# A two-block transformer with a mixture of experts on one core: retention on 128-token tiles, a spread slot product, and fetched tokens in place of one-hot gathers

## The chip, the core and the metric

The kernel runs on one core of a Trainium2 chip. The metric is device time in microseconds of one execution; the profile is of one such execution. PE is the matmul engine, PEld its weight loads, DVE, ACT and POOL the vector, scalar and general engines, SP the engine that issues most of the DMAs.

## The reference

Two blocks follow each other on one sequence of 512 tokens of width 1024. The first mixes tokens by windowed attention and by retention, then by a convolution, each followed by attention over a memory. The second has three branches and then a mixture of 32 experts, two per token. The parts that the change touches:

```python
def retention(q, k, v):                      # 4 heads, key and value width 128, CHUNK = 64
    intra = jnp.exp(log_gamma[:, None, None] * jnp.abs(idx[:, None] - idx[None, :]))
    k_decay = jnp.exp(log_gamma[:, None] * (CHUNK - 1 - idx)[None, :])
    q_decay = jnp.exp(log_gamma[:, None] * (idx + 1.0)[None, :])
    chunk_decay = jnp.exp(log_gamma * CHUNK)
    sc = jnp.einsum('bnihd,bnjhd->bnhij', qc, kc) * intra
    o_intra = jnp.einsum('bnhij,bnjhe->bnihe', sc, vc)
    kv = jnp.einsum('bnjhd,bnjhe,hj->nbhde', kc, vc, k_decay)
    _, states = lax.scan(lambda state, kv_c: (state * chunk_decay + kv_c, state), 0, kv)
    o = o_intra + jnp.einsum('bnihd,nbhde,hi->bnihe', qc, states, q_decay)
    return o * lax.rsqrt(jnp.mean(o * o, axis=-1, keepdims=True) + EPS)

def hierarchical_moe(h, ...):                # router, then per expert: tokens in, tokens out
    weights, expert_idx = ...                # two experts of each token, and their weights
    def run_block(toks, e):
        xb = x_pad[toks]
        a = jax.nn.silu(xb @ w_gate_e[e]) * (xb @ w_up_e[e])
        return a @ w_down_e[e]
    y = yb.reshape(R, D) * row_w[:, None]
    return jax.ops.segment_sum(y, row_tok)
```

## The kernel before

Features lie on partitions and tokens on the free axis; a big product is three float32r matmuls (high and low parts of weights and data, L321 to L323). Weights come from HBM by SP into two buffers `raw`, and ACT and DVE split each half (`w`, L250 and L251, three buffers). Up to the experts a scheduler sets the order of all engines from the program and its priorities; in the experts (`moe`) PE's order is as written, and the other engines are still scheduled. Every engine runs its list in order.

**Retention** (`retention`, L572) runs for two heads after the first half of its projections (the calls are in the loop `for half in range(2)`) and for two after the second. On a tile of 128 tokens the scores are one product (L577), masked by `intra` to two blocks of 64; `kd` is k transposed (L584) and scaled on ACT (L586). Then come 7 products of 64 rows for the chunk states (L592), 7 steps on DVE that chain the states (L597), 8 products of 64 columns with them (L602), 4 inner products (L608), and the normalization, after which `retention_out` transposes `oc` (L627). The gate projection of the same half (`ew` group 3 or 7) stands beside it on PE. In the second half ACT and DVE also prepare the memory (`ms`, L253 and L254, from POOL's product L418) and the first weights of the next stage (`w` from `in_wkv`).

**The experts.** Each of the 32 experts has 64 slots in the first round; expert j and j + 16 share a tile of 128 rows. A turn i of `moe` handles tiles a = 2i and b = 2i + 1: `gu` (L1398, gate and up, 32 matmuls of 512 columns on 64 of them at a time), `act`, `flip` (transposes of the 128 x 256 result, L1412), `down` (L1424), and `combine` of the turn before (L1445), which adds the rows back to their tokens. Weights of a turn are twelve loads of 1 MB into a ring of twelve tiles `ew` (four for `gu` of a, four for b, two and two for `down`); each is loaded again as soon as PE is through with it. The tokens of a turn come by `gather(i)`, called between `flip` and `down` of b in the turn before (and once ahead of the loop): either 64 float32r matmuls of the kept activations `h2` with one-hot matrices `oh` that DVE builds (L1347, L1348, L1364), or, for i in `FETCH` = 3, 5, 7, rows of the copy `hd` in HBM that POOL fetched by two indirect DMAs of 128 rows each (`fetch`, L1332) and that PE transposes (L1358). `slot_rows` (L1281) makes for each slot its token, its weight and its norm: 8 steps of five small DVE operations and one float32 product of 48 columns (L1295). It stands after `gu` of tile 0, and `act` of tile 0 needs its result `rh`; the fetches need its `sti`.

## Time and profile before

| | |
|---|---|
| median of 3 runs | 1682.16 us (1681.27 to 1683.08) |
| profiled execution, its own time | 1682.74 us |
| its span, first to last instruction | 1680.8 us |
| PE busy over the span | 1622.0 us (97%) |
| 157 to 252 us (retention of both halves): PE busy | 90.1 of 95 us |
| 252 to 1358 us: PE busy | 1100.2 of 1106 us |
| 1358 to 1681 us (experts and end): PE busy | 287.2 of 323 us |
| bytes moved, whole span | 237.7 MB, 141 GB/s |
| bytes per second, 1358 to 1681 us | 318 GB/s, DMA engines busy 0.79 |

A row of the timeline gives start, length, engine, line, operation, output and inputs, shape and count; what stands in brackets is the idle time of the engine ahead of it and who ended it. Matmuls overlap: a length is longer than the distance to the next start, and it is the distance that counts. A float32 matmul shows as two instructions. A granted clock of 1.00 is 2.4 GHz, one of 0.50 is 1.2 GHz.

### The profile page before, as it was taken

The page shows a single profiled execution, that of the slowest core. Times are in us where ns is not written, and L with a number is a line of the kernel's source. Part 1 is how long each engine was busy: PE and PEld are TensorE (multiplying, and loading weights), DVE is VectorE, ACT ScalarE, POOL GpSimd, SP SyncE. Part 2 cuts the span into 40 slices and gives each one's busy share as a digit, 9 for nine tenths or more (in the row PEclk, how much of TensorE's full clock was granted, in tenths as well). Part 3 has the DMA queues.
Part 4 walks back from the last instruction along what each step waited for, and adds up shares of the span by engine and source line. Part 5 has one row for each costly group of instructions (what it writes and reads, how often), then busy time and mean ns, then how long its engine had stood idle before and what let it go on. Part 6 is the DMA issues. An engine that isn't in the chain of part 4 may idle for free. (4 is left out here: it accounts for less than half of the span.)

```text
span 1680.8 us, 20780 instructions
## 1 busy us (share of the span) xinstructions
PE 1622.0 (97%) x8174; PEld 1239.3 (74%) x8174; DVE 917.3 (55%) x1745; ACT 588.8 (35%) x1036; POOL 117.7 (7%) x104
## 2 busy tenths in 40 slices
PE   7999999999999999999999999999999968999995
PEld 6757769888888889888877777888888854545542
DVE  5575755545555465555795554475445453434335
ACT  5443234435322234434545443245333311111112
POOL 0000200000011120000030000000111200000001
PEclk9999989999999999999999999999999978999998
DMA  6211125220322235230231112242432367899981
GB/s 205 100 51 51 51 79 197 101 75 30 108 88 101 101 116 185 103 124 26 100 110 52 52 58 95 94 163 84 177 125 101 91 231 317 354 382 369 397 361 52
DMA packets 43368, 237.73 MB, mean 141 GB/s; under 512 B 6128, under 2 KB 11120, under 8 KB 17152
## 3 DMA queue, kind: packets, MB, share of 16 engines
q1 hardware_dynamic: 41088, 228.93, 36.6%
q0 software_dynamic: 2176, 7.41, 1.3%
q8 instruction: 66, 1.08, 0.3%
q14 instruction: 38, 0.31, 0.1%
HBM read 230.03 MB, written 6.29 MB: 141 GB/s over the span
## 5 line engine op out<-in xcount | busy, mean ns | idle before, releaser
L250 ACT ACTIVATE w<-raw 128x1024 fp32r<-128x1024 f32 (+2 forms) x242 | 233.9, 968 | 398.5 <-PE mm L323 354.9
L321 PE MATMUL mm<-xg,w 128*128 128x512 f32 x864 | 342.0, 396 | 9.7 <-ACT xg L253 8.0
L251 DVE TENSOR_TENSOR w<-raw,w 128x1024 fp32r<-128x1024 f32 (+2 forms) x242 | 280.5, 1160 | 124.0 <-ACT w L250 122.8
L322 PE MATMUL mm<-xg,w 128*128 128x512 f32 x864 | 341.0, 395 | 0.0
L323 PE MATMUL mm<-xg,w 128*128 128x512 f32 x864 | 340.5, 394 | 0.0
L321 PEld LDWEIGHTS mm<-xg,w 128*128 128x128 f32 x864 | 163.1, 189 | 45.3 <-ACT xg L253 8.0
L323 PEld LDWEIGHTS mm<-xg,w 128*128 128x128 f32 x864 | 163.1, 189 | 35.6 <-issue 3.0
L322 PEld LDWEIGHTS mm<-xg,w 128*128 128x128 f32 x864 | 163.1, 189 | 34.7 <-issue 2.5
L322 PE MATMUL mm<-y,w 128*128 128x512 f32 x448 | 175.3, 391 | 0.0
L323 PE MATMUL mm<-y,w 128*128 128x512 f32 x448 | 174.1, 389 | 0.0
L321 PE MATMUL mm<-y,w 128*128 128x512 f32 x448 | 174.0, 391 | 0.0
L1398 PE MATMUL pgu<-ew,xT 128*64 128x512 f32 x512 | 115.6, 605 | 0.0
L321 PEld LDWEIGHTS mm<-y,w 128*128 128x128 f32 x448 | 83.8, 188 | 18.1 <-ACT y L250 1.2
L323 PEld LDWEIGHTS mm<-y,w 128*128 128x128 f32 x448 | 84.1, 188 | 17.3
L322 PEld LDWEIGHTS mm<-y,w 128*128 128x128 f32 x448 | 84.1, 188 | 17.0 <-DVE y L251 0.4
L1398 PEld LDWEIGHTS pgu<-ew,xT 128*64 128x64 f32 x512 | 36.5, 139 | 72.9 <-issue 71.8
L1445 PE MATMUL py<-ys,comb 128*128 128x512 f32 x256 | 62.4, 397 | 0.0
L1424 PE MATMUL py<-ew,aT 128*64 128x512 f32 x256 | 58.1, 595 | 0.7 <-ACT aT L1414 0.7
L1445 PEld LDWEIGHTS py<-ys,comb 128*128 128x128 f32 x256 | 46.8, 188 | 16.1 <-issue 5.7
L1405 DVE SCALAR_TENSOR_TENSOR eth<-eth,pgu 128x256 f32<-128x256 f32 x16 | 6.7, 421 | 94.2 <-ACT eth L1404 94.2
L1404 ACT ACTIVATE eth<-pgu,rh 128x256 f32<-128x256 f32 x16 | 7.6, 475 | 139.8 <-PE pgu L1398 124.3
L1447 DVE TENSOR_TENSOR merged<-py,merged 128x512 f32<-128x512 f32 x64 | 44.1, 690 | 10.6 <-PE py L1445 10.1
(438 smaller groups left out, 2499.4 us busy)
## 6 DMA issues: line engine op xcount, KB each, us to landing
ew<-in_egu_dram SPq DMA_DIRECT2D x64, 1024.0 KB, 8.5
ew<-in_edn_dram SPq DMA_DIRECT2D x32, 1024.0 KB, 10.2
raw<-in_wkv_dram SPq DMA_DIRECT2D x20, 1024.0 KB, 4.8
raw<-in_ow_dram SPq DMA_DIRECT2D x16, 1024.0 KB, 4.7
raw<-in_ew_dram SPq DMA_DIRECT2D x12, 1024.0 KB, 4.8
raw<-in_w2gate_dram SPq DMA_DIRECT2D x12, 1024.0 KB, 4.8
raw<-in_wq_dram SPq DMA_DIRECT2D x8, 1024.0 KB, 4.8
raw<-in_wo_dram SPq DMA_DIRECT2D x8, 1024.0 KB, 4.8
```

Source lines behind the costliest of these rows:

```text
L250: nc.scalar.activation(hi, src, AF.Copy)
L251: nc.vector.tensor_tensor(lo, src, hi.bitcast(F32), op=ALU.subtract)
L321: nc.tensor.matmul(ps, lhsT=lh, rhs=rh, start=first, stop=False)
L322: nc.tensor.matmul(ps, lhsT=lh, rhs=rl, start=False, stop=False)
L323: nc.tensor.matmul(ps, lhsT=ll, rhs=rh, start=False, stop=last)
L1398: nc.tensor.matmul(ps[64 * i:64 * i + 64], lhsT=xT[k][:, o + 64 * i:o + 64 * i + 64], rhs=W[2 * (k // 4) + i][:, k % 4], start=k == 0, sto ...
L1404: nc.scalar.activation(th, pg_[:, :256], AF.Tanh, scale=rh[:, j:j + 1])
L1405: STT(th, th, 1.0, pg_[:, :256], op0=ALU.add, op1=ALU.mult)
L1424: nc.tensor.matmul(py[64 * i:64 * i + 64], lhsT=aT[:, f, 64 * i:64 * i + 64], rhs=W[i][:, f, n * 512:n * 512 + 512], start=f == 0, stop=f ...
L1445: nc.tensor.matmul(py, lhsT=comb[:, t * 128:t * 128 + 128], rhs=y[:, c], start=i == 0, stop=i == len(parts) - 1)
L1447: TT(xts[t][:, c], py, xts[t][:, c], op=ALU.add)
```

## The change

Three edits. First, retention works on tiles of 128 tokens: the mask also lets the second 64 tokens of a tile see the first 64 (`sees` in place of `same`), the decays count 128 tokens, and per head there are 3 state products with all 128 rows, 2 chain steps on DVE (the first state is a copy on ACT), and 3 products of all 128 columns; the inner product now comes ahead of them, ACT copies it, and DVE adds the scaled cross term to three of the four tiles. Second, `slot_rows` becomes a generator: `gather(0)` calls two of its steps after each of its four groups of 16 matmuls, its result sits in a `py` bank, and in turn 0 both `gu` follow each other, with `flip` of a after them. Third, `FETCH` is 1 to 7: only `gather(0)` is a one-hot product; each turn fetches for the next one.

```diff
-FETCH, AHEAD = (3, 5, 7), 2
+FETCH = range(1, 8)
...
-    same = (p[:, None] // 64) == (p[None, :] // 64)
+    sees = (p[:, None] // 64) <= (p[None, :] // 64)
...
-    put("kdec", np.stack([np.exp(g * (63 - i)) * scale for g in lg], 1))
-    put("qdec", np.stack([np.exp(g * (i + 1.0)) for g in lg], 1))
+    put("kdec", np.stack([np.exp(g * (127 - p)) * scale for g in lg], 1))
+    put("qdec", np.stack([np.exp(g * (p + 1.0)) for g in lg], 1))
...
-            st = f4("st").rearrange("p (c e) -> p c e", c=8)
-            nc.vector.memset(st[:, 0], 0.0)
-            pk = [scps(), scps()]
-            for c in range(7):
-                p0, t = 64 * (c % 2), c // 2
-                nc.tensor.matmul(pk[c % 2][:, t * 128:t * 128 + 128],
-                                 lhsT=kd[p0:p0 + 64, t * 128:t * 128 + 128],
-                                 rhs=v[p0:p0 + 64, t, vo:vo + 128], start=True, stop=True)
-            for c in range(7):
-                t = c // 2
-                nc.vector.scalar_tensor_tensor(st[:, c + 1], st[:, c], CDECAY[h],
-                                               pk[c % 2][:, t * 128:t * 128 + 128], op0=ALU.mult, op1=ALU.add)
-            pc = trps()
-            for c in range(8):
-                p0, t = 64 * (c % 2), c // 2
-                nc.tensor.matmul(pc[p0:p0 + 64, t * 128:t * 128 + 128], lhsT=q[:, c * 64:c * 64 + 64],
-                                 rhs=st[:, c], start=True, stop=True)
-            oc = f2("oc")
-            nc.scalar.activation(oc, pc, AF.Copy, scale=qdec[:, h:h + 1])
+            st = f2("st").rearrange("p (t e) -> p t e", t=4)
+            pk = scps()
+            for t in range(3):
+                c = slice(t * 128, t * 128 + 128)
+                nc.tensor.matmul(pk[:, c], lhsT=kd[:, c], rhs=v[:, t, vo:vo + 128], start=True, stop=True)
+            nc.scalar.activation(st[:, 1], pk[:, :128], AF.Copy)
+            for t in (1, 2):
+                nc.vector.scalar_tensor_tensor(st[:, t + 1], st[:, t], CDECAY[h], pk[:, t * 128:t * 128 + 128],
+                                               op0=ALU.mult, op1=ALU.add)
             pi = scps()
...
-            nc.vector.tensor_tensor(oc, oc, pi, op=ALU.add)
+            pc = trps()
+            for t in range(1, 4):
+                c = slice(t * 128, t * 128 + 128)
+                nc.tensor.matmul(pc[:, c], lhsT=q[:, c], rhs=st[:, t], start=True, stop=True)
+            oc = f2("oc")
+            nc.scalar.activation(oc, pi, AF.Copy)
+            nc.vector.scalar_tensor_tensor(oc[:, 128:], pc[:, 128:], qdec[:, h:h + 1], oc[:, 128:], op0=ALU.mult,
+                                           op1=ALU.add)
...
-    def gather(j2):
+    def gather(j2, between=lambda: None):
...
+            between()
             x_ = xs[:, f2_ % 2]
...
-        xT = gather(0)
+        steps = slot_rows(pq.tile([128, 512], F32, name="py", tag="py", bufs=3)[:, :48])
+        def two():
+            for _ in range(2):
+                next(steps, None)
+        xT = gather(0, two)
+        next(steps, None)
...
-            if i + AHEAD in FETCH:
-                fetched[i + AHEAD] = fetch(i + AHEAD)
+            if i + 1 in FETCH:
+                fetched[i + 1] = fetch(i + 1)
             pa = gu(a, xT, wga)
...
-            if i == 0:
-                rows()
             ta = act(a, pa)
-            out_ = combine(last) if i else iter(())
-            for _ in range(2):
-                next(out_, None)
-            aT = flip(ta)
+            if i:
+                out_ = combine(last)
+                for _ in range(2):
+                    next(out_)
+                aT = flip(ta)
...
             tb = act(b, pb)
+            if not i:
+                aT = flip(ta)
```

The scheduler moves other work with it. On PE, at the first head of the second half (line numbers of each kernel's own file; `mm` is the gate projection that fills in, `tr<-st` the cross product, `sc<-bv,kd` the state product, `sc<-bv,rPT` the inner product), before:

```order
L577 MATMUL sc<-rot 128x128 x4
L584 MATMUL tr<-ident,rot 128x128 x4
L602 MATMUL tr<-st,rot 64x128
L321 MATMUL mm<-xg,w 128x512
L322 MATMUL mm<-xg,w 128x512
L323 MATMUL mm<-xg,w 128x512
L592 MATMUL sc<-bv,kd 128x128 x7
L584 MATMUL tr<-ident,rot 128x128 x4
L321 MATMUL mm<-xg,w 128x512
L322 MATMUL mm<-xg,w 128x512
L602 MATMUL tr<-st,rot 64x128
```

and with the change:

```order
L577 MATMUL sc<-rot 128x128 x4
L584 MATMUL tr<-ident,rot 128x128 x4
L321 MATMUL mm<-xg,w 128x512
L322 MATMUL mm<-xg,w 128x512
L323 MATMUL mm<-xg,w 128x512
L321 MATMUL mm<-xg,w 128x512
L592 MATMUL sc<-bv,kd 128x128 x3
L599 MATMUL sc<-bv,rPT 128x128 x4
L604 MATMUL tr<-st,rot 128x128
L584 MATMUL tr<-ident,rot 128x128 x4
L577 MATMUL sc<-rot 128x128
L604 MATMUL tr<-st,rot 128x128 x2
```

The cross products now stand together, directly behind the state and inner products, where single ones alternated with `mm`.

On ACT at the same place (`ms` is the memory, `bv` the values, `kd` the scaled keys, the `w` right behind `kd` the split of the next stage's first weights from `in_wkv`), before:

```order
L253 ACTIVATE ms<-raw,vec 128x256 x4
L250 ACTIVATE w<-raw 128x1024
L733 ACTIVATE bv<-mm,r_tok 128x256 x4
L586 ACTIVATE kd<-tr,kdec 128x512
L250 ACTIVATE w<-raw 128x1024
L605 ACTIVATE oc<-tr,qdec 128x512
```

and with the change:

```order
L253 ACTIVATE ms<-raw,vec 128x256 x7
L250 ACTIVATE w<-raw 128x1024
L253 ACTIVATE ms<-raw,vec 128x256
L731 ACTIVATE bv<-mm,r_tok 128x256 x4
L586 ACTIVATE kd<-tr,kdec 128x512
L250 ACTIVATE w<-raw 128x1024
L593 ACTIVATE st<-sc 128x128
L606 ACTIVATE oc<-sc 128x512
```

The new copy of the first state (`st`) stands behind the split of the `in_wkv` weights, and three more `ms` operations and a fourth stand ahead of `bv`.

On PE at the start of the experts (`h` with a number is one of the eight kept activations, `pg` the gathered tokens, `rv,lh` the slot product, `pgu` gate and up), before:

```order
L1364 MATMUL pg<-oh,h_10520 128x256 x8
L1364 MATMUL pg<-oh,h_10570 128x256 x8
L1398 MATMUL pgu<-ew,xT 64x512 x16
L1295 MATMUL pg<-rv,lh 128x48 x8
L1412 MATMUL pat<-ident,eth 128x128 x2
L1398 MATMUL pgu<-ew,xT 64x512 x16
L1424 MATMUL py<-ew,aT 64x512 x8
L1412 MATMUL pat<-ident,eth 128x128 x2
```

and with the change:

```order
L1363 MATMUL pg<-oh,h_10460 128x256 x8
L1363 MATMUL pg<-oh,h_10510 128x256 x8
L1293 MATMUL py<-rv,lh 128x48 x2
L1398 MATMUL pgu<-ew,xT 64x512 x32
L1412 MATMUL pat<-ident,eth 128x128 x2
L1424 MATMUL py<-ew,aT 64x512 x8
L1412 MATMUL pat<-ident,eth 128x128 x2
L1357 MATMUL pg<-ident,xg 128x128 x16
```

The slot product is gone from between the two `gu`, which now stand as one row of 32, and the next gather is 16 transposes of fetched tokens. On POOL the six indirect fetches of the experts become fourteen; SP's list is the same.

## Rows read from the trace of the kernel before

**Rows 1.** Busy time by stretch: the two halves of retention, from the first score product to the end of the half (the first up to the scores of the second; the second up to the four transposes of `oc`). Columns: stretch, length, then busy time and count of PE, PEld, DVE, ACT and POOL, granted clock, DMA share, GB/s.

```profile
156.83:209.04 52.21, 50.17 (x301) 39.33 (x300) 37.50 (x76) 14.36 (x21) 12.44 (x8) 1.00 0.14 51
209.04:243.63 34.59, 31.82 (x154) 21.09 (x153) 16.82 (x52) 8.97 (x15) 0.00 (x0) 0.85 0.22 82
```

**Rows 2.** Timeline of PE, retention of the first half: two plain projections, scores and transposes, state products, and cross products (L602) between projections.

```profile
151.39 0.39 PE L321 MATMUL mm<-xg,w 128*128 128x512 f32 x1
151.62 0.39 PE L322 MATMUL mm<-xg,w 128*128 128x512 f32 x1
...
156.83 1.05 PE L577 MATMUL sc<-rot 128*128 128x128 f32 x8
157.72 0.60 PE L584 MATMUL tr<-ident,rot 128*128 128x128 f32 x4
...
159.51 1.16 PE L592 MATMUL sc<-bv,kd 64*128 64x128 f32 x14
160.60 0.66 PE L584 MATMUL tr<-ident,rot 128*128 128x128 f32 x4
...
162.57 0.49 PE L323 MATMUL mm<-xg,w 128*128 128x512 f32 x1
163.00 0.43 PE L602 MATMUL tr<-st,rot 128*64 128x128 f32 x2
163.36 0.49 PE L321 MATMUL mm<-xg,w 128*128 128x512 f32 x1
```

**Rows 3.** Timeline of PE, retention of the second half: the wait of the first dependent cross product and what follows.

```profile
213.55 0.40 PE L322 MATMUL mm<-xg,w 128*128 128x512 f32 x1
216.72 0.43 PE L602 MATMUL tr<-st,rot 128*64 128x128 f32 x2 [2.77 <-DVE st L597]
...
221.74 0.80 PE L321 MATMUL mm<-xg,w 128*128 128x512 f32 x1
...
228.34 0.50 PE L322 MATMUL mm<-xg,w 128*128 128x512 f32 x1
```

**Rows 4.** Busy time by stretch behind that wait, columns as in rows 1.

```profile
215.00:220.00 5.00, 3.29 (x10) 1.56 (x11) 3.14 (x8) 0.21 (x1) 0.00 (x0) 0.81 0.00 0
220.00:225.00 5.00, 5.00 (x14) 2.58 (x14) 0.00 (x0) 0.46 (x1) 0.00 (x0) 0.50 0.00 0
225.00:230.00 5.00, 5.00 (x25) 3.96 (x25) 3.17 (x8) 2.22 (x5) 0.00 (x0) 0.67 0.00 0
```

**Rows 5.** Timeline of ACT and then of DVE around the same wait.

```profile
214.15 1.06 ACT L250 ACTIVATE w<-raw 128x1024 fp32r<-128x1024 f32 x1 [2.89 <-DMA raw<-in_wkv_dram]
...
208.21 1.21 DVE L251 TENSOR_TENSOR w<-raw,w 128x1024 fp32r<-128x1024 f32 x1
...
215.24 1.23 DVE L251 TENSOR_TENSOR w<-raw,w 128x1024 fp32r<-128x1024 f32 x1 [4.41 <-ACT w L250]
216.38 2.21 DVE L597 SCALAR_TENSOR_TENSOR st<-st,sc 128x128 f32<-128x128 f32 x7
```

**Rows 6.** Waits of PE in the first half: who waited for whom, us in total, times, longest.

```profile
PE tr L627 <- DVE oc L620: 2.0, 2, 1.2
```

**Rows 7.** Timeline of PE at the start of the experts: one-hot gather, `gu` of tile 0, the slot product's steps, `flip`, `gu` of tile 1, `down`.

```profile
1370.34 10.27 PE L1364 MATMUL pg<-oh,h 128*128 128x256 f32 x64 [2.99 <-DVE oh L1348]
1380.54 7.09 PE L1398 MATMUL pgu<-ew,xT 128*64 128x512 f32 x32
1387.56 0.65 PE L1295 MATMUL pg<-rv,lh 128*128 128x48 f32 x4
...
1391.14 0.42 PE L1295 MATMUL pg<-rv,lh 128*128 128x48 f32 x2 [0.52 <-DVE rv L1294]
1392.08 0.51 PE L1295 MATMUL pg<-rv,lh 128*128 128x48 f32 x2 [0.52 <-DVE rv L1294]
...
1396.74 0.69 PE L1412 MATMUL pat<-ident,eth 128*128 128x128 f32 x2 [2.16 <-DVE eth L1406]
1397.36 9.63 PE L1398 MATMUL pgu<-ew,xT 128*64 128x512 f32 x32
1406.83 3.60 PE L1424 MATMUL py<-ew,aT 128*64 128x512 f32 x16
```

**Rows 8.** Timeline of PE at the end of the last turn, where `down` follows `flip` with nothing between.

```profile
1651.73 0.44 PE L1412 MATMUL pat<-ident,eth 128*128 128x128 f32 x2
1652.89 3.65 PE L1424 MATMUL py<-ew,aT 128*64 128x512 f32 x16 [0.72 <-ACT aT L1414]
```

**Rows 9.** Busy time by stretch for turns 1 to 3, each from the start of its first `gu`; turns 1 and 3 hold a one-hot gather, turn 2 a gather from fetched rows. Columns as in rows 1.

```profile
1421.89:1458.62 36.73, 36.73 (x199) 20.73 (x196) 15.29 (x32) 5.56 (x10) 0.00 (x0) 1.00 0.85 344
1458.62:1490.15 31.53, 31.20 (x151) 14.73 (x149) 12.45 (x22) 5.45 (x10) 1.87 (x2) 1.00 0.88 355
1490.15:1526.83 36.68, 36.68 (x198) 20.73 (x196) 14.60 (x28) 5.56 (x10) 0.00 (x0) 1.00 0.99 409
```

**Rows 10.** Busy time by stretch where the DMA engines are never idle, with a fetch in the first stretch and without in the second. Columns as in rows 1.

```profile
1485.00:1510.00 25.00, 24.67 (x116) 12.07 (x116) 10.46 (x19) 3.23 (x6) 1.87 (x2) 1.00 1.00 412
1510.00:1525.00 15.00, 15.00 (x100) 10.12 (x98) 5.36 (x11) 3.32 (x6) 0.00 (x0) 1.00 1.01 419
```

**Rows 11.** Time from issue to landing of the six indirect fetches, and then of the `gu` weights issued in turn 3.

```profile
DMA to landing us min/median/max: 4.6/9.2/11.9
...
DMA to landing us min/median/max: 7.7/11.9/16.1
```

More of the change, by code (lines that the diff above doesn't have):

```diff
@@ L46, in _constants @@
     lg = np.log1p(-np.exp2(-5.0 - np.arange(4)))
-    i = p % 64
-    same = (p[:, None] // 64) == (p[None, :] // 64)
+    sees = (p[:, None] // 64) <= (p[None, :] // 64)
     scale = 128.0 ** -0.5
-    put("intra", np.stack([np.where(same, np.exp(g * np.abs(p[:, None] - p[None, :])), 0.0) * scale for g in lg], 1))
-    put("kdec", np.stack([np.exp(g * (63 - i)) * scale for g in lg], 1))
-    put("qdec", np.stack([np.exp(g * (i + 1.0)) for g in lg], 1))
+    put("intra", np.stack([np.where(sees, np.exp(g * np.abs(p[:, None] - p[None, :])), 0.0) * scale for g in lg], 1))
+    put("kdec", np.stack([np.exp(g * (127 - p)) * scale for g in lg], 1))
+    put("qdec", np.stack([np.exp(g * (p + 1.0)) for g in lg], 1))
     c = np.arange(256)
@@ L73, in _constants @@
         o += a.shape[1]
-    return np.ascontiguousarray(np.concatenate(list(cols.values()), 1)), off, [math.exp(g * 64) for g in lg]
+    return np.ascontiguousarray(np.concatenate(list(cols.values()), 1)), off, [math.exp(g * 128) for g in lg]
 CONST, COFF, CDECAY = _constants()
@@ L1296, in slot_rows @@
                                  stop=k == 1 and t == 3)
+                yield k, t
         nc.vector.tensor_copy(rh, ps[:, 16:32])
@@ L1471, in finish @@
         nc.sync.dma_start(o[:, :H], y[:, :H])
-    def rows():
-        slot_rows(pq.tile([128, 512], F32, name="pg", tag="pg", bufs=2)[:, :48])
     def moe():
         wga, wgb, wda, wdb = load_gu(0), load_gu(1), load_dn(0), load_dn(1)
-        xT = gather(0)
+        steps = slot_rows(pq.tile([128, 512], F32, name="py", tag="py", bufs=3)[:, :48])
[4 more added lines that the diff above has]
+        next(steps, None)
         last = []
@@ L1488, in moe @@
                 wga = load_gu(a + 2)
-            if i == 0:
-                rows()
             ta = act(a, pa)
-            out_ = combine(last) if i else iter(())
-            for _ in range(2):
-                next(out_, None)
-            aT = flip(ta)
-            for _ in out_:
-                pass
+            if i:
[3 more added lines that the diff above has]
+                aT = flip(ta)
+                for _ in out_:
+                    pass
             pb = gu(b, xT, wgb)
```

## The prediction

> **What bounds the kernel now.** I read the page first: PE is busy 97% of the span, so time goes where PE works or waits, and the three edits must be priced on PE. The page's chain of work that ended last covers only a few per cent of the span and does not lead back to either place, so I used the busy time by stretch, then PE's timeline, then the waits. In the two halves of retention PE is hardly idle (2.0 us of 52.2, 2.8 of 34.6) [rows 1], so what counts there is how much of PE's time the products take. The reader is to see three things. A plain projection starts 0.23 us after the one before it (151.39 to 151.62); a projection with one cross product L602 behind it takes 0.79 us (162.57 to 163.36) [rows 2]. So a lone 64-column product costs 0.56 us. In the second half PE stands 2.77 us for the chain of states, and after it the granted clock is at 1.2 GHz until about 228 us [rows 3, 4]. In the experts PE alternates between turns of 36.7 us with a one-hot gather and 31.53 us with a fetched one [rows 9]; and turn 0 has a hole, 9.8 us from the first slot product (1387.56) to the second `gu` (1397.36), which then takes 9.63 us where the first took 7.0 [rows 7].
>
> **Retention.** Per half (two heads) it loses 16 cross products at 0.56 us, 9.0 us, and two groups of seven state products at 1.09 us (159.51 to 160.60), 2.2 us [rows 2]. It gains 6 + 6 float32 products with all 128 rows and columns. The nearest row is the four score products, same shape, which take 0.89 us (156.83 to 157.72), 0.22 us each [rows 2]: 2.7 us. They now stand together, and neither the scores nor the transposes, of the same shape, slow the work beside them. Net 8.5 us per half at 2.4 GHz.
>
> Waits in the first half. The 2.0 us for `oc` [rows 6] mostly go, since the transposes stand further behind the chain. New ones come: `kd` is one ACT operation behind the transposes, about 0.3 us a head uncovered, and the last two cross products wait for two chain steps on DVE, between the small operations of the other head's normalization. I estimate 1.5 us in all. Net: 9.0 us saved, between 6.5 (the old wait stays and the new ones come) and 10.5 (no wait left).
>
> Second half. Of its 34.6 us [rows 1], 2.8 are the wait and 5.1 the clock: the three stretches of 5 us lack 0.19, 0.50 and 0.33 of it [rows 4]. Full-speed work is 26.7 us, with the change 18.2. But the wait's cause is not removed. DVE's chain stood behind the split of the next stage's weights, which waited on ACT, which waited 2.89 us for the load from `in_wkv`; that load starts when another split (208.21 + 1.21 us) frees its buffer [rows 5]. Now the first state is a copy on ACT behind the same split, and three more `ms` operations stand ahead of the freeing split. PE has less to do until then: scores, transposes, four projections, state and inner products, some 4.3 us from 209.04, so it comes to the first cross product at 213.4. The split ends at 215.2, or 216.1 if the load starts 0.9 us later; with the copy PE waits 2.4 to 3.2 us. With the chain steps behind DVE's split I take 3.2 in all. Whether the clock falls again is the largest unknown. Nothing (the wait just misses it) and 5.1 us (as before) are the ends; I take 3.1, as dense work follows now, and the one-hot gather, dense after a wait of 2.99 us, lost only about 2.3 us (10.2 us against the 7.9 us that turns 1 and 3 leave for it: 36.7 less 31.53 and some 2.7 for the fetched kind) [rows 7, 9]. Then this half is 18.2 + 3.2 + 3.1 = 24.5 us: 10 us saved, of which I keep 9, for `bv` and so the state products come later behind the added `ms`. Bounds 6 and 14. Retention: 18 us, bounds 12.5 and 24.5.
>
> A rule speaks against this edit. The Trainium skill (TensorE: Matmul & The Clock Gate, Part 3: Packing small matmuls) says that products on different row or column parts of the array run at the same time, which is what halves of 64 allow. The state products agree: seven in 1.09 us, 0.16 each against 0.22. By the rule the sixteen cross products would cost about 2.5 us and the edit save 2 us a half rather than 8.5. The cross products do not show it, as each stands alone between projections.
>
> **Slot product and turn 0.** The hole closes. Eight steps move into the gather: two took 0.65 us together, one 0.42, so about 0.23 us more each on PE [rows 7], 1.8 us in all. Their DVE work paced them at 0.94 us a step (1391.14 to 1392.08), 7.5 us; beside a gather of 10.2 us with two buffers it nearly hides. Ends: 1.8 us (all hidden) and 7.5 (none); I take 2.5, nearer the first, since the gather's 16 products between two calls take 2 to 4 us and two steps on DVE 1.9. So the second `gu` starts at 1387.56 + 2.5 = 1390.1, lasts 7.0 and ends at 1397.1. `flip` of a now stands bare ahead of `down`; in the last turn that cost 1.16 us from start to start (1651.73 to 1652.89) [rows 8]. `down` starts at 1398.2 in place of 1406.83: 8.6 us saved, 3.6 to 9.3 by those ends. `act` of a lies under the second `gu`, for `rh` is ready soon after the gather. POOL's first fetch can issue at about 1386 and lands at most 11.9 us later [rows 11], at 1398; its transposes come at about 1402.
>
> **Fetches.** Four gathers change kind, each worth 36.7 - 31.53 = 5.2 us [rows 9]: 20.7 us. POOL issues the next fetch when the transposes free its buffers, some 3.5 us before the turn starts, and it is needed 25.5 us into the turn; a landing of 11.9 us hides. On SP nothing moves. What this cover hangs on is the DMA. A turn now moves 13 pieces of 1.05 MB, 13.6 MB in 31.53 us, 432 GB/s; the saturated stretch with a fetch moved 412 [rows 10], 33.1 us a turn. So the loads fall back 1.5 us a turn, 9 us over six turns. They have that room: a tile is loaded again half a `gu` after its use and needed a turn later, 28 us, and the longest landing in turn 3, itself saturated, was 16.1 us [rows 9, 11]. 16.1 + 9 = 25.1: the room holds, by 3 us. I take 0.
>
> **Sum.** 18 + 8.6 + 20.7 = 47.3 us off the profiled execution's 1682.74 us: 1635.4, say **1635.5**. That execution is 0.6 us above the median of the runs, so the same holds against 1682.16. Between the two places PE is busy 1100 of 1106 us and loads there follow PE, so a gain in retention is kept.
>
> **Rivals.**
> The forecast, chance 0.65: 1628 to 1642.
> *DMA becomes the bound*, 0.19. The loads use up their 28 us and PE waits in the last turns. At 400 GB/s a turn is 34.1 us, 2.6 behind, 15 over six turns against 12 of room: 3 us lost; at 380, 36 us a turn, 26 behind: 14 lost. So 1639 to 1650, and PE's waits would name `in_egu` or `in_edn`. For it: a forecast room of only 3 us. Against: 419 GB/s without a fetch [rows 10]. A page goes further: the Trainium skill (DMA: Bandwidth & Descriptors, Where 436 GB/s comes from) says "For HBM↔SBUF transfers the HBM side (~358) binds". By that figure a turn would take 38 us and the fetches give nothing, about 1660 to 1665; the saturated rows, at 412 and 419, do not bear it out.
> *Retention gives half*, 0.13. The wait for `in_wkv` is longer than the old one, the clock stays at 1.2 GHz for all of the second half's remaining 15 us or so, and the first half trades its old wait for as much new: 9 us in place of 18, 1642 to 1647.
> *Slower*, 0.02. The fetch, issued one turn ahead in place of two, arrives after its transposes; PE stands in each gather and the clock falls, which costs about 2.6 us each time (9.63 against 7.0) [rows 7]. To eat 47 us over seven gathers each must be 4 us late, so a landing of 33 us; then 1682.7 and more. The longest seen is 11.9 [rows 11].
> *Nothing changes*, 0.01: were `FETCH` or the spread not in effect; the listed order shows both.
>
> **Range.** The low end joins retention's upper part (no fall of the clock, 4 us) with the hidden slot product and the lost waits: 1627. The high end takes in the second rival's middle and most of the third: 1648. About 0.85 of the chance lies inside by these cases. Within 0.2%, 3.4 us, is about what a measurement here can tell from no change: faster 0.97, same 0.01, slower 0.02.
>
> **What would show it.** Right: the second half of retention near 25 us; cross products 0.2 to 0.3 us apart; no slot product after the first `gu`, and `down` of turn 0 some 8.6 us earlier relative to the start of the gather; turns 1 to 6 at 31.5 us each; landings of `ew` growing from turn to turn to 20 to 25 us. Wrong: PE waits for `in_egu`, `in_edn` or `hd` in the experts, turns above 32 us, a granted clock below 1.00 after 1400 us, or a wait of over 4 us behind `in_wkv`.

## The result and the profile after

| | before | after |
|---|---|---|
| median | 1682.62 us (4 runs, 1681.27 to 1683.54) | 1633.31 us (4 runs, 1631.04 to 1634.57) |
| ratio | | 0.9706, 95% interval 0.9689 to 0.9723 |
| span of the profiled execution | 1680.8 us | 1631.6 us |
| PE busy | 1622.0 us (97%) | 1576.8 us (97%) |
| bytes moved | 237.7 MB | 241.9 MB |

The change takes 49.3 us off (interval 46.6 to 52.3); 47.3 were forecast, and 1633.31 lies 2.2 us from the predicted 1635.5. The whole span, cut at the same instructions in both kernels, shows where they came from (us; the cuts are starts on PE that stand in the rows here, in [rows 1], [rows 7] and in [rows 8]; the last `down` of the kernel after starts at 1605.43):

| stretch | before | after | difference | forecast |
|---|---|---|---|---|
| start to the first score product | 156.83 | 157.74 | +0.91 | 0 |
| first half of retention | 52.21 | 43.79 | -8.42 | -9 |
| second half, to the first product with `ms` | 34.59 | 24.78 | -9.81 | -9 |
| from there to the first gather | 1126.71 | 1126.65 | -0.06 | 0 |
| first gather to `down` of turn 0 | 36.49 | 27.30 | -9.19 | -8.6 |
| from there to the last `down` | 246.06 | 225.17 | -20.89 | -20.7 |
| last `down` to the end | 27.91 | 26.17 | -1.74 | 0 |
| sum | 1680.80 | 1631.60 | -49.20 | -47.3 |

The first and last lines are scatter between executions rather than an effect: up to the first score product PE has the same 682 matmul records in both kernels, and in the executions profiled below, with the same work there, the first stretch took 156.3 to 158.9 us and the last 26.0 to 27.4 us, whether a kernel held this edit or that; the 27.91 us of the kernel before stand just outside.

Busy time by stretch of the kernel after: both halves of retention (to be read against [rows 1]), the first gather with turn 0, and turns 1 and 6 (against [rows 9]). Columns: stretch, length, then busy time and count of PE, PEld, DVE, ACT and POOL, granted clock, DMA share, GB/s.

```profile
157.74:201.53 43.79, 42.30 (x265) 37.20 (x264) 33.58 (x68) 15.34 (x25) 14.39 (x8) 1.00 0.17 59
201.53:226.31 24.78, 21.28 (x122) 18.39 (x121) 15.26 (x47) 9.30 (x18) 0.00 (x0) 0.93 0.32 117
1352.96:1380.26 27.30, 26.25 (x146) 16.10 (x146) 13.72 (x64) 2.42 (x5) 2.02 (x2) 0.92 0.84 333
1390.19:1421.68 31.49, 31.16 (x150) 14.73 (x148) 12.45 (x22) 5.45 (x10) 1.88 (x2) 1.00 1.01 419
1547.64:1579.13 31.49, 31.16 (x151) 14.72 (x148) 12.44 (x22) 5.45 (x10) 0.00 (x0) 1.00 1.01 419
```

Three things are to be seen. What the first half of retention lost is nearly all work of PE, 7.9 us (50.17 to 42.30), and only 0.5 us of waits. Turns 1 to 6 take 31.49 us, each of them, with the DMA engines never idle. And the second half of retention still has 3.5 us of idle PE and a mean clock of 0.93.

PE's timeline of the first head: inner and cross products and the next head's scores, which answer to [rows 2]; then the wait in the second half, which answers to [rows 3].

```profile
160.97 1.06 PE L599 MATMUL sc<-bv,rPT 128*128 128x128 f32 x8
161.86 0.83 PE L604 MATMUL tr<-st,rot 128*128 128x128 f32 x6
162.53 1.06 PE L577 MATMUL sc<-rot 128*128 128x128 f32 x8
...
209.14 0.49 PE L604 MATMUL tr<-st,rot 128*128 128x128 f32 x2 [3.25 <-ACT st L593]
```

Three cross products now take 0.67 us from start to start (161.86 to 162.53), 0.22 each, where eight at 0.56 took 4.5. In the second half PE stands 3.25 us for the first state, the copy on ACT. ACT's timeline and the clock behind the wait (against [rows 5] and [rows 4]):

```profile
207.87 1.06 ACT L250 ACTIVATE w<-raw 128x1024 fp32r<-128x1024 f32 x1 [3.86 <-DMA raw<-in_wkv_dram]
208.83 0.26 ACT L593 ACTIVATE st<-sc 128x128 f32<-128x128 f32 x1
```

```profile
205.00:210.00 5.00, 1.75 (x16) 1.56 (x15) 1.04 (x1) 1.71 (x3) 0.00 (x0) 1.00 0.92 387
210.00:215.00 5.00, 4.86 (x25) 4.33 (x24) 2.57 (x6) 1.32 (x2) 0.00 (x0) 0.66 0.01 3
```

The copy starts as soon as the split has ended that waited for `in_wkv`. PE then works at a mean granted clock of 0.66 for 5 us, which loses 1.7 us.

PE's timeline at the start of the experts (against [rows 7]): the first and the second group of the gather with the slot products between them, both `gu` as one row, `flip`, `down`.

```profile
1352.96 4.16 PE L1363 MATMUL pg<-oh,h 128*128 128x256 f32 x16 [2.98 <-DVE oh L1347]
1356.91 0.49 PE L1293 MATMUL py<-rv,lh 128*128 128x48 f32 x2
...
1358.17 2.15 PE L1363 MATMUL pg<-oh,h 128*128 128x256 f32 x16
...
1365.43 13.95 PE L1398 MATMUL pgu<-ew,xT 128*64 128x512 f32 x64
1379.32 0.44 PE L1412 MATMUL pat<-ident,eth 128*128 128x128 f32 x2
1380.26 3.65 PE L1424 MATMUL py<-ew,aT 128*64 128x512 f32 x16 [0.51 <-ACT aT L1414]
```

The gather with its eight slot steps takes 12.47 us (1352.96 to 1365.43) against 10.20 without them: 2.27 us for steps that had left PE 9.8 us from `gu` to `gu`. Both `gu` run at full clock.

How near the DMA came to its bound shows on SP. SP's waits in the experts (who, for whom, us in total, times, longest), and then, of turn 6, the last of the four `gu` loads of tile a for turn 7: its issue, and the time to its landing.

```profile
SPq L1380 <- DMA ew<-in_egu_dram: 31.5, 15, 3.4
SPq L1388 <- DMA ew<-in_egu_dram: 16.6, 12, 2.1
SPq L1380 <- DMA ew<-in_edn_dram: 14.9, 8, 2.5
```

```profile
L1380 SPq DMA_DIRECT2D ew<-in_egu_dram x1: 328/328/328, 1560.5 to 1560.5; - x1
...
DMA to landing us min/median/max: 20.0/20.0/20.0
```

In the kernel before, SP's weight loads waited in the experts almost only for PE, which frees their tiles (0.5 us, once, for an earlier load). Now they waited 63 us for earlier loads to land. The tile of that last load was free when the first `gu` of turn 6 ended, at 1554.6; the load was issued 5.9 us later and landed at 1580.5, and PE wanted it halfway through the first `gu` of turn 7, at 1582.6. So 25.9 of 28 us of room were used, and 2.1 us were left. The same load took 20.9 us from free tile to landing in turn 1, and then 22.0, 22.9, 23.8 and 24.7: some 1.0 us more each turn.

### The profile page after: what moved, and what is told of

The parts are those of the page before. It is cut to its first block, busy times and chain, and to the rows that moved or that the text cites. A ratio compares the mean times of both kernels' runs of the same rounds, so it can differ in the third digit from the quotient of the medians.

```text
span 1631.6 us, 20208 instructions
## 1 busy us (share of the span) xinstructions
PE 1576.8 (97%) x7910; PEld 1209.0 (74%) x7910; DVE 897.7 (55%) x1681; ACT 588.6 (36%) x1040; POOL 127.0 (8%) x112
## 5 line engine op out<-in xcount | busy, mean ns | idle before, releaser
L321 PEld LDWEIGHTS mm<-y,w 128*128 128x128 f32 x448 | 83.8, 188 | 18.2 <-ACT y L250 1.2
L390 DVE TENSOR_TENSOR x<-mm,x 128x512 f32<-128x512 f32 x32 | 22.1, 691 | 50.6 <-PE mm L323 50.6
```

Of the source, the lines that this page charges most:

```text
L321: nc.tensor.matmul(ps, lhsT=lh, rhs=rh, start=first, stop=False)
L390: nc.vector.tensor_tensor(x[:, m], ps, x[:, m], op=ALU.add)
```

## The experiments

The theory is that of the prediction: each edit acts at its own place on PE, and nothing between gives a gain back. The rivals are told with each run. Experiments 1 to 3 take the edits one by one, 4 takes the wait away, 5, 6, 7 and 12 price the cross product, 8 loads the DMA, 9 gives the kernel before a new order of its cross products and nothing else, and 10 and 11 try a faster start of the experts. All times are medians; the kernel before took 1682.1 to 1683.4 us beside them.

### 1 to 3: one edit at a time

Experiment 1 holds the constants and `retention` of the change and nothing else; experiment 2 holds `slot_rows`, `gather` and the order of turn 0; experiment 3 has this:

```diff
-FETCH, AHEAD = (3, 5, 7), 2
+FETCH = range(1, 8)
...
-            if i + AHEAD in FETCH:
-                fetched[i + AHEAD] = fetch(i + AHEAD)
+            if i and i + 1 in FETCH:
+                fetched[i + 1] = fetch(i + 1)
...
                 rows()
+                fetched[1] = fetch(1)
```

> Only the first edit (retention on 128-token tiles) on the kernel before. Theory A (each edit acts at its own place and what lies between follows PE, so the gains add): the stretch from the first score product to the first product of the memory stage gets about 17 us shorter, as in the changed kernel (from 86.8 to 68.6 us there, with four projections moved ahead of it), and the time is 1682.6 - 17.4 = 1665 us. Rival B (part of the retention gain needs the later edits, or the loads in between take some of it back): 1669 to 1674 us, with PE waits that the changed kernel does not have between 250 and 1350 us.

> Only the second edit (slot products spread through the first gather, both gate-and-up passes of turn 0 together, flip of tile a behind them), with one-hot gathers and fetches for turns 3, 5 and 7 as before. Theory A: 9.2 us, as in the changed kernel, where the stretch from the first gather product to down of turn 0 went from 36.5 to 27.3 us: 1673.4 us. Rival B (the one-hot work that DVE builds for turn 1 in the same stretch competes with the slot steps, so that the gather takes longer than the 12.5 us of the changed kernel): 3 to 6 us only, 1676 to 1680 us.

> Only the third edit (tokens of turns 1 to 7 fetched one turn ahead); the slot products stay behind the first gate-and-up pass, and the first fetch is issued right behind them. Theory A: four gathers at 5.2 us, 20.8 us: 1661.8 us; every turn takes 31.5 us. Rival B (the fetch of turn 1 now starts some 7 us later against its use and PE stands for it in turn 0): 2 to 4 us less gain, 1664 to 1666 us, and PE waits for the fetched rows in turn 0.

| | time, us | ratio (95%) | gain | its own stretch: before, alone, all three |
|---|---|---|---|---|
| 1 retention | 1661.78 | 0.9879 (0.9863 to 0.9896) | 20.3 | 86.80, 68.76, 68.57 |
| 2 slot steps | 1674.75 | 0.9953 (0.9936 to 0.9969) | 7.4 | 36.49, 29.13, 27.30 |
| 3 fetches | 1659.31 | 0.9867 (0.9850 to 0.9884) | 22.8 | 246.06, 225.17, 225.17 |

The three gains add to 50.5 us, against 49.3 for all: theory A, within the intervals. No projection moved ahead of retention, as the expectation of experiment 1 has it: the counts up to the first score product are equal. Its time fell 2.3 us more than its stretch; the stretch between retention and the experts took 1123.0 to 1128.0 us in the executions profiled here, which covers that. Experiment 3 shows no wait of PE for fetched rows though its first fetch starts behind the slot steps, so its rival falls. In experiment 2 the stretch is 1.8 us longer than in the changed kernel, but not through DVE, as rival B had it. PE's timeline of the first two groups of the gather, and the busy time of their stretches:

```profile
1372.72 4.15 PE L1365 MATMUL pg<-oh,h 128*128 128x256 f32 x16 [2.99 <-DVE oh L1349]
...
1378.14 3.76 PE L1365 MATMUL pg<-oh,h 128*128 128x256 f32 x16
```

```profile
1372.72:1376.72 4.00, 3.96 (x17) 3.67 (x18) 4.00 (x19) 0.00 (x0) 0.00 (x0) 0.50 1.02 430
1376.72:1380.72 4.00, 3.48 (x17) 3.32 (x17) 2.63 (x16) 0.60 (x1) 0.00 (x0) 0.50 1.01 426
```

The second group of 16 takes 3.76 us at a clock of 0.50 where it took 2.15 in the changed kernel; the products and waits are the same. So the low clock behind PE's waits of 8.7 and 3.0 us lasts longer in one execution than in another. The short form is the rarer one: of eight executions with this start of the experts (the changed kernel and experiments 2, 4 to 8 and 12) two have it, with 27.3 us from the gather to `down`, and six took 28.9 to 29.5 us.

### 4: the load behind the wait, started earlier

```diff
+        raw = spare("raw8") if spare else wr.tile([128, 2048], F32, name="raw", tag="raw")
...
+    kT, vM = even_layer(n0, n1, lambda: mem_kv(..., spare=f8))
...
-            proj_fm(wload(w[gi], 8, 256), ch, ek, 2 * gi, n=M)
+            proj_fm(wload(w[gi], 8, 256, spare if gi == 0 else None), ch, ek, 2 * gi, n=M)
```

> The changed kernel, with the first in_wkv weights of the memory stage loaded into the 8 KB buffer that window attention has given up, in place of one of the two load buffers: the load no longer waits for a split to free its buffer. Theory A (the wait of 3.25 us in the second half of retention is that load, and the low clock behind it is that wait): both go, 3.25 us and about 1.7 us, so 1633.3 - 5 = 1628.4 us, and the granted clock stays at 1.00 from 200 to 230 us. Rival B (the states are late for another reason, DVE's list or the products before them, so that the wait finds another releaser): 0 to 2 us, 1631.5 to 1633.5 us. Rival C (the clock falls at this place whatever the wait): 3.3 us, 1630 us, with a clock below 1.00 left at 210 us.

`spare` is a buffer of 8 KB that window attention has given up. The kernel took 1627.07 us (1625.50 to 1629.89; ratio to before 0.9668, 0.9651 to 0.9684; the changed kernel's is 0.9706). Busy time of the second half, and of the two stretches where the changed kernel stood and then ran slowly; then what PE still waited for in both halves:

```profile
200.94:221.04 20.10, 19.27 (x122) 16.73 (x121) 15.50 (x47) 9.35 (x18) 0.00 (x0) 1.00 0.28 105
```

```profile
205.00:210.00 5.00, 5.00 (x42) 4.63 (x41) 3.22 (x11) 2.16 (x5) 0.00 (x0) 1.00 0.83 344
210.00:215.00 5.00, 5.00 (x30) 4.37 (x29) 4.03 (x18) 1.50 (x3) 0.00 (x0) 1.00 0.01 3
```

```profile
PE tr L625 <- DVE oc L618: 1.4, 1, 1.4
PE sc L592 <- ACT kd L586: 0.8, 1, 0.8
```

The wait for the first state is gone, the clock stays at 1.00, and the half takes 20.10 us in place of 24.78, with a small new wait for `kd`: theory A. Rival C falls: the clock did not fall where PE had not waited. This version beats both kernels.

### 5, 6, 7 and 12: what a cross product costs

Each adds sixteen float32 products to the gate projection of the first half, where nothing else is disturbed:

```diff
                     mm3(ps, hi[:, k - a], lo[:, k - a], rhs[k][0], rhs[k][1], k == 0, k == KK - 1)
+                    extra()
...
+                po, q0, k0, n = pops(), qh[0], kh[0], [0]
...
+                def extra():
+                    for _ in range(1):
+                        p0 = 64 * (n[0] % 2) if 64 == 64 else 0
+                        nc.tensor.matmul(po[p0:p0 + 64, :128], lhsT=q0[:, :64], rhs=k0[:, :128], start=True, stop=True)
+                        n[0] += 1
```

This is experiment 5. Experiment 6 has `lhsT=q0[:, :128]` and writes all 128 partitions of `po`, 7 makes sixteen products at one place (`range(16)`), and 12 is 7 with `p0 = 0`.

> The changed kernel with sixteen float32 products of 64 columns added to the gate projection of the first half, one behind each third projection (operands from the rotated q and k, result in the idle bank po, never read). It prices the lone cross product of the kernel before by itself. Theory A (what cost 0.56 us was a 64-column product that stands alone between projections): 0.56 us each, about 9.0 us, 1642 us. Rival B (the 0.56 us came from what the cross products waited for, their states and banks, and a product alone costs as much as one in a group): 0.2 to 0.25 us each, 3.5 to 4 us, 1637 us.

> As e5_lone64, but each added product has all 128 columns. Theory A1 (the price is that of standing alone, whatever the columns): 0.56 us each again, 9 us, 1642 us. Theory A2 (the price is that of 64 columns): about 0.22 us each as in a group, 3.5 us, 1637 us.

> As e5_lone64, but the sixteen products of 64 columns stand in one group behind one projection, even ones into the lower and odd ones into the upper 64 partitions of the bank. Theory A1 (standing alone costs): 0.22 us each and 0.3 us once for the change of kind, 3.8 us, 1637 us. Theory A2 (64 columns cost): 0.5 us each, 8 us, 1641 us. Rival R (products on different halves run at the same time, as the 64-row state products did at 0.16 us each): 0.11 to 0.16 us each, 1.8 to 2.6 us, 1635.5 us. If R holds, a version that kept 64-token chunks but let the cross products stand together would have given nearly all of the gain.

> As e7_group64, but all sixteen products of 64 columns go to the lower 64 partitions of the bank, one after another. Theory R (in e7_group64 the 0.12 us came from neighbours on different halves running at the same time): about 0.22 us each, 3.5 us for the group in place of 1.9. Rival S (a 64-column product in a group takes 0.12 us whatever half its neighbour uses): 1.9 us again.

PE's timeline and its weight loads' (PEld) around one product alone with 64 columns (experiment 5):

```profile
146.34 0.39 PE L323 MATMUL mm<-xg,w 128*128 128x512 f32 x1
146.66 0.43 PE L741 MATMUL po<-rot 128*64 128x128 f32 x2
...
147.92 0.43 PE L741 MATMUL po<-rot 128*64 128x128 f32 x2
...
146.66 0.19 PEld L741 LDWEIGHTS po<-rot 128*64 128x64 f32 x2 [0.36 <-issue]
147.02 0.19 PEld L321 LDWEIGHTS mm<-xg,w 128*128 128x128 f32 x1 [0.17 <-issue]
```

and with 128 columns (experiment 6):

```profile
146.39 0.39 PE L323 MATMUL mm<-xg,w 128*128 128x512 f32 x1
146.61 0.38 PE L741 MATMUL po<-rot 128*128 128x128 f32 x2
...
147.53 0.39 PE L741 MATMUL po<-rot 128*128 128x128 f32 x2
...
146.39 0.41 PEld L741 LDWEIGHTS po<-rot 128*128 128x128 f32 x2
```

The distance from one added product to the next, less three projections of 0.23 us, is its price: 1.26 - 0.69 = 0.57 us with 64 columns (146.66 to 147.92), 0.92 - 0.69 = 0.23 us with 128 (146.61 to 147.53). What makes the difference is in PEld's rows. The 64-column weights are loaded only at 146.66, the product's own start, 0.36 us after the end of the load before, and the next load, of 128 columns, comes late again, after 0.17 us. The 128-column weights are loaded while the projection ahead runs (146.39, where the product starts at 146.61). So A2, but with a narrower reading: standing alone costs nothing, a change between 64 and 128 columns from one neighbour to the next does. Why the load waits there, the trace does not show. The groups, in experiment 7 (alternating halves) and then in 12 (lower half only):

```profile
154.45 1.97 PE L742 MATMUL po<-rot 128*64 128x128 f32 x32
156.35 0.50 PE L321 MATMUL mm<-xg,w 128*128 128x512 f32 x1
```

```profile
154.54 3.71 PE L742 MATMUL po<-rot 128*64 128x128 f32 x32
158.18 0.50 PE L321 MATMUL mm<-xg,w 128*128 128x512 f32 x1
```

Sixteen take 1.90 us on alternating halves, 0.12 each, and 3.64 us on one half, 0.23 each: the rival R of experiment 7, and 64 columns by themselves cost no more than 128. This is what the Trainium skill says (TensorE: Matmul & The Clock Gate, Part 3: Packing small matmuls): products on different parts of the array run at the same time. The cross products of the kernel before could not use it, since 128-column projections stood between them. The times, of one run each, stand in the same order: 1640.70 us for experiment 5, 1635.01, 1634.20 and 1635.46 for 6, 7 and 12. Each is 1 to 2 us less than 1633.31 and its price, which single runs cannot tell from scatter (the changed kernel's own runs lie between 1631.0 and 1634.6).

### 9: 64-token chunks, cross products together

```diff
-            for c in range(8):
-                p0, t = 64 * (c % 2), c // 2
-                nc.tensor.matmul(pc[p0:p0 + 64, ...
+            with tc.high_priority():
+                for c in reversed(range(8)):
+                    p0, t = 64 * (c % 2), c // 2
+                    mm = nc.tensor.matmul(pc[p0:p0 + 64, ...
+                    if c < 7:
+                        tc.keep_in_program_order(mm)
```

> The kernel before with one thing changed: the eight cross products of a head stand in one group (written from the last state to the first, each pinned behind the one before), still 64-token chunks, 64 columns each, alternately in the lower and upper half of the bank. Theory A (from e5 to e7: the 0.56 us is paid where a 64-column product has 128-column neighbours; in a group, on alternating halves, one costs 0.12 us): a head pays 8 x 0.12 + 0.3 = 1.3 us in place of 4.5, so 3.2 us less for each of four heads, 13 us: 1669.5 us; the larger tiles as such are then worth only the rest of the 17 to 20 us. Rival B (the larger tiles are what saves, by fewer products and chain steps; moved together, the products wait longer for the last of seven chain steps and lose what they save): 0 to 5 us, 1677 to 1682 us.

It took 1667.68 us, ratio 0.9913 (0.9897 to 0.9930): 15.3 us less than the kernel before, by an edit that only orders its 32 cross products; the scheduler moved projections and inner products around them. PE's timeline of the cross products of one head, and of the wait in the second half:

```profile
163.49 1.09 PE L603 MATMUL tr<-st,rot 128*64 128x128 f32 x16
164.52 0.71 PE L611 MATMUL sc<-bv,rPT 128*128 128x128 f32 x4
...
214.61 0.49 PE L611 MATMUL sc<-bv,rPT 128*128 128x128 f32 x2 [2.87 <-DVE st L597]
```

Eight cross products take 1.03 us. From the first score to the first `ms` product (157.01 to 231.26) it is 74.25 us: 12.6 of the change's 18.2 us come with the order alone. The halves are not alike, because of the clock. The first gives 3.9 us (48.28 for 52.21), with a granted clock of 0.96 where it was 1.00, behind a wait of 2.2 us for `oc`; the second gives 8.6 us (25.97 for 34.59), with 0.93 where it was 0.85. At an even clock I estimate 11 us from these numbers. The wait of 2.87 us in the second half stays. Theory A; rival B's dearer wait for the last state does not show.

### 8: more load on the DMA

```diff
+        for i in range(2):
...
+            spare = xy.tile([128, D], F32, name="xd", tag="xd")
+            nc.gpsimd.indirect_dma_start(out=spare, out_offset=None, in_=hd, in_offset=off)
```

> The changed kernel with every fetch made twice, the second time into a spare tile that nobody reads (for its 4 KB the gathered tokens have two buffers in place of three, and POOL's order in the experts is as written). It loads the DMA beyond what the change does. Theory A (a weight may land up to 28 us after its issue before PE waits, and PE does not wait in the changed kernel because its longest landing stays below that): 14.68 MB a turn at 419 GB/s take 35.0 us, 3.5 us more than a turn; landings start at about 18 us and grow by 3.5 us a turn, so the first turns cost nothing, and from about the fourth each costs up to 3.5 us, 10 to 13 us in all: 1643 to 1647 us, with PE waits for in_egu or in_edn of that sum. Rival B (the changed kernel stands at its edge already): every turn pays, 21 to 25 us, 1655 us and more. Rival C (the loads have more room than 28 us, or the chip moves more than 419 GB/s): under 3 us, 1633 to 1636 us.

It took 1648.27 us (ratio 0.9795, 0.9778 to 0.9811), 15.0 us more than the changed kernel. The first row is PE's waits for `in_egu` in turns 1 to 7, the second those of its weight loads for them, which stop a little earlier than the products; the others are PE's timeline where two of the waits fell:

```profile
PE pgu L1402 <- DMA ew<-in_egu_dram: 7.4, 3, 2.5
```

```profile
PEld pgu L1402 <- DMA ew<-in_egu_dram: 11.1, 6, 3.4
```

```profile
1458.44 5.34 PE L1402 MATMUL pgu<-ew,xT 128*64 128x512 f32 x14 [2.44 <-DMA ew<-in_egu_dram]
...
1528.38 3.65 PE L1402 MATMUL pgu<-ew,xT 128*64 128x512 f32 x14 [2.49 <-DMA ew<-in_egu_dram]
```

Turns 1 and 2 still take 31.5 us; turns 3 to 6 take 36.7, 33.2, 35.1 and 36.7. So theory A: the room pays for the first turns, and then PE waits for `in_egu`. Turns 3 to 6 are 15.7 us longer than four of 31.49. Of this, 3.4 us are the clock, which the forecast of 10 to 13 us did not have: behind two of the three longest waits, in turns 3 and 6, 14 products took 5.34 in place of 3.65 us, at a granted clock of 0.95 over the turn. The other 12.3 us are waits for loads, as PEld shows them (11.1 us for `in_egu`, and 0.9 for `in_edn`); turns 4 and 5 are longer at a clock of 1.00.

### 10 and 11: a warm start of the first gather

```diff
+    def warm(n):
+        ps = mmps()
+        for _ in range(n):
+            tc.keep_in_program_order(nc.tensor.matmul(ps, lhsT=h2[0][0][:, :128], rhs=h2[1][0], start=True, stop=True))
```

> The kernel of e4_wkv with 41 products of 512 columns added whose result nobody reads: 30 in PE's wait of 8.7 us ahead of the routing sums, 11 in its wait of 3.0 us ahead of the first gather. They are to keep the granted clock at 1.00 when the first gather starts; in the changed kernel its first 16 products ran at 0.50 and took 4.16 us where the next 16 took 2.15. Theory A (the clock is what the start of the gather loses): the first 16 take 2.15 us; but DVE's slot steps were ready only at about 1356.9, when the slow products ended, so PE waits there for most of the 2 us: 0 to 1 us gained, plus up to 1.4 us against executions in which the low clock lasts into the second 16: 1625.5 to 1627 us. Rival B (the added products delay the routing sums or the gather): 1628 to 1630 us.

> As e10_warm, with no slot step behind the first group of 16 gather products, two behind the second and three behind each of the last two, so that PE does not stand for DVE's first slot steps. Theory A: the 2 us of the clock now arrive, less what three steps (2.8 us on DVE) hold up the last two groups (2.15 + 0.7 us on PE): 1 to 2 us less than e4_wkv, 1625 to 1626 us. Rival B (DVE's eight steps of 0.94 us set the end of the gather wherever they stand): as e10_warm or slower.

They took 1627.63 us (1627.23 to 1629.50) and 1628.98 us (1626.48 to 1630.84): no gain on experiment 4. PE's timeline of the first gather group in experiment 10, and its busy time:

```profile
1349.18 0.80 PE L1370 MATMUL pg<-oh,h 128*128 128x256 f32 x4 [0.36 <-DVE oh L1354]
1350.40 1.85 PE L1370 MATMUL pg<-oh,h 128*128 128x256 f32 x12 [0.42 <-DVE oh L1354]
1352.74 0.42 PE L1299 MATMUL py<-rv,lh 128*128 128x48 f32 x2 [0.49 <-DVE rv L1298]
```

```profile
1349.00:1353.00 4.00, 2.92 (x18) 2.41 (x18) 3.90 (x18) 0.60 (x1) 0.00 (x0) 1.00 1.01 426
```

The clock is 1.00 from the start, and PE now waits for DVE, busy 3.90 of 4 us; the first group with its waits takes 3.56 us in place of 3.95. So DVE sets the pace of the first group, and takes back most of the 2 us. From the gather to `down` it is 26.9 us, 0.4 less than in the changed kernel; against the six executions in which the low clock reached the second group it is 2 us less, but the times of four runs do not show that. Experiment 11 moved the waits behind the last groups (PE stood 0.95 and 1.42 us there for `rv`), and behind the second of them the granted clock fell again, to 0.57 for 4 us, so that the two `gu` took 15.65 us for 13.95. So rival B of experiment 11 holds, by DVE's pace and by a low clock behind the moved wait.

## Why the prediction was right

**The sum.** Each of the three edits gave what its term said, each at its own place, and they add (experiments 1 to 3). That the gain in retention survives 1126 us of PE-bound work is shown by the table, 1126.71 and 1126.65 us, to within the 2 to 3 us by which this stretch differs between executions; that the two agree to 0.06 us is chance.

**Retention, first half.** It gave 8.4 us for 9.0. The new products cost what the score products do, as taken, and PE's work fell by 7.9 us for 8.5. The waits come to 1.5 us, as estimated, but not those that were named: the wait for `oc` was to go and stays with 1.36 us, and the new ones for `kd` and the chain steps are 0.1 us in all. That part of the sum is luck.

**Retention, second half.** It gave 9.8 us for 9, and 3.4 of them are the clock (5.1 us lost before, 1.7 after). The wait stayed, with 3.25 us for 3.2, at the place and with the cause that were named, as experiment 4 shows by taking it away. The other two sizes missed in opposite directions and cancel, which is luck: the clock cost 1.7 us for 3.1, and the work at full clock, 24.8 less 3.5 idle and 1.7 for the clock, is 19.6 us for 18.2. Of this 0.4 us are transposes of `oc`, of which eight now lie inside the stretch where there were four; the rest stays open.

**The price of a cross product** was right and its reason only half right. 0.56 us is what one costs between projections (0.57 in experiment 5), but not because it stands alone: one of 128 columns there costs 0.23. The text gave "They now stand together" as what makes the new ones cheap; their 128 columns would have done it alone. The rule of packing, which the prediction set against the edit, agrees with experiments 7 and 12 (0.12 and 0.23 us) and was no objection to the edit, since the cross products did not stand where it acts; but it pointed at a cheaper edit, and experiment 9 got 12.6 of the 18.2 us with it.

**Turn 0.** It gave 9.2 us for 8.6. The slot steps cost 2.27 us for 2.5, within the bounds of 1.8 and 7.5, and `flip` to `down` 0.94 for 1.16. This too is in part luck of the two executions that were profiled: with the old start the stretch took 36.5 us here and 35.4 to 35.6 in experiments 1, 3 and 9, with the new one 27.3 here and 28.9 to 29.5 in six of eight, as the clock went. The other pairs give 6 to 8 us, nearer to experiment 2's 7.4 and still within 3.6 to 9.3. The prediction took what the clock costs in the gather as the same before and after.

**Fetches.** They gave 20.9 us for 20.7, and no turn takes more than 31.49 us.

**The room of the loads** is where the forecast was closest to failing. The fall behind was priced by a rate of 412 GB/s; the experts ran at 419. Landings were to grow to 20 to 25 us, and stopped at 22.4; that looks like more room than foreseen and is not, for the rest of the delay moved to SP, which waited for earlier loads before it issued the next. From a free tile to its landing it was 25.9 us in turn 6, for a forecast of 25.1 and a room of 28. Two misses cancel in this: the start was 20.9 us in turn 1 where 16.1 had been taken from turn 3 of the kernel before, and the growth was 1.0 us a turn for 1.5. With 1 MB more a turn, experiment 8, the rival of the DMA came true: PE waits for `in_egu` from turn 3 on, and 15 us are lost. The Trainium skill (DMA: Bandwidth & Descriptors, Where 436 GB/s comes from) has the HBM side bind at some 358 GB/s, which it gives as one core's half of an HBM stack. Turns 1 to 6, on the one core of this program, ran at 419 and do not show that limit.

## What to carry to other kernels

Before counting a small product by its flops, look at its neighbours: where the column count changed from one product to the next, here between 64 and 128, the weight load no longer hid, 0.57 us in place of 0.12 to 0.23, and putting equal products together was worth most of a larger rewrite. A ring of loads that fell behind showed first in the waits of the engine that issues, and only later in PE's; landing times alone looked nearly settled while the room ran out by 1 us a turn. And when a wait goes, or a clock is kept up, ask which engine stands right behind: in the first group of the gather DVE took back most of what the clock would have given. One profile is one draw: where the clock falls, look at the same stretch in several executions before giving it a price.

## What was not expected of the hardware

- Weights of 64 columns behind a product of 128, and the reverse, were loaded only 0.36 and 0.17 us after the end of the load before (experiment 5); with equal columns the load followed at once and ran under the product ahead (experiment 6).
- SP's issue of a 1 MB load waited up to 3.4 us for an earlier load to land, 63 us in all in the changed kernel, and the time from issue to landing did not pass 22.4 us there, and 25.0 in experiment 8, where the loads came too late for PE. Whether the queue or the order of waits in the program holds the issue back, the trace does not show.
- The granted clock behind the same wait differs from one execution to the next: at the first gather it stayed at 0.50 for 4 us in the changed kernel and for 8 us in experiment 2, with the same products and waits; that alone is 1.6 us. Six of eight executions had the longer form.
